# An attention stage in a two-layer encoder: the values matmul with its operands exchanged, two heads on two halves of the array, and the softmax's divisors spread over partitions

## The chip, the cores and the metric

The kernel runs on one core of one Trainium2 chip. A core has a matrix engine (TensorE, PE in the profile, with its weight loads listed apart as PEld), a vector engine (VectorE, DVE), a scalar engine (ScalarE, ACT) and a general engine (GpSimd, POOL); SyncE (SP) issues most of the transfers. Each engine works through its own queue in order, and they wait for each other by semaphores. The metric is the time of one execution on the device in microseconds, lower is better.

## The reference

Two layers; each one takes x of 512 tokens by 1024 features through a half-weighted SwiGLU, a mixer, a second half-weighted SwiGLU and a norm. The mixer has two groups side by side, attention and a causal depthwise convolution of 31 taps, and one output projection over both. What matters here is the end of the attention:

```python
        scores = jnp.where(allowed[None, None], scores, -1e30)
        probs = jax.nn.softmax(scores, axis=-1).astype(vs.dtype)
        outs.append(jnp.einsum('bhqk,bhkd->bqhd', probs, vs))
    ...
    out = jnp.concatenate(outs, axis=1)
    return out.reshape(b, s, h * V_DIM)
    ...
    x = x + jnp.concatenate([attn, conv], axis=-1) @ w_out[l]
```

There are 8 heads with values of 64 columns. Queries come in blocks of 128 tokens; block i sees the keys of blocks 0 to i, with a mask inside the last block. Everything is float32.

## The kernel before

The activations lie transposed, features on partitions and tokens in the free dimension, in tiles of 128x512. Large products keep float32 accuracy by splitting both operands into a high and a low float32r part and adding three matmuls (`mm3`, lines 154 to 156); this fills most of the span. Attention's own small products are single float32 matmuls.

In `mix_body` the attention runs head by head in stages, written down as `ORDER = "t0s1p3v4o5"`: at step n the kernel issues the turning of head n (`turn`, t), the scores of head n-1 (`scores`, s), the turning of the probabilities of head n-3 (`turn_p`, p), the values of head n-4 (`values`, v) and the turning of the output of head n-5 (`turn_out`, o). A scheduler then orders each engine's queue from these and from the convolution, which is issued beside them. So the written order is not the final one.

The stages around the change:

- `scores` makes, for each block of 128 queries, one matmul of up to 512 keys (L834), the mask as a small bf16 matmul (L835), a maximum on DVE (L836) and an exponential on ACT (L840) whose row sums go to `sums`, queries on partitions. The probabilities aren't divided here.
- `turn_p` transposes the probabilities, 10 blocks of 128x128 a head (L855), and copies them out of PSUM on DVE or ACT (L858), so that keys lie on partitions: `pt[j]` holds key block j and the queries of blocks j to 3.
- `values` multiplies them with the values `vs[j]` (L868): for each query block t and key block j up to t, weights are `pt[j]`'s 128 queries, and the moving operand is the head's 64 columns of `vs[j]`. That is 10 matmuls a head. The result has queries on partitions. For an odd head it also makes 1/sum on DVE (`rs`, L873) and multiplies both heads' results by it (`o`, L875).
- `turn_out` transposes the pair's result with four transposes (L886) into a tile with the two heads' features on partitions, and `split` makes its high and low parts (cast on ACT, L161; subtraction on DVE, L162). Four such tiles are the attention's part of the output projection's operand.

The convolution runs over the same stretch. Of four channel blocks two are made on DVE (L922); for the other two ACT makes each tap's product (L926, three buffers) and POOL adds it (L930). When all four are done, POOL adds them up (L944 to L946), PE sums that over the channels (L948), and DVE and ACT normalize. In PE's queue L948 stands before all matmuls of the output projection; the sums of the squares (L198) come two groups of the projection later.

Of the kernel before, what the change touches and what calls it, by code (L numbers as in the profile page):

```python
# [12 lines left out]
ALU = mybir.AluOpType  # L13
AX = mybir.AxisListType

P = 128
# [4 lines left out]
NT = S // P  # L21
# [4 lines left out]
DV = 64  # L26
# [48 lines left out]
def encoder_kernel(ctx: ExitStack, tc: tile.TileContext, xT, consts, vecs, rgain, wgu1, wd1, wdq1,  # L75
# [11 lines left out]
    def nm(s):  # L87
        uid[0] += 1
        return f"{s}{uid[0]}"
# [4 lines left out]
    def tmp(w=S, dt=FP):  # L94
        return tmps.tile([P, w], dt, tag="t", name=nm("t"))

    def bank():
        return psum.tile([P, S], FP, tag="ps", name=nm("ps"))
# [4 lines left out]
    V, A, G, T = nc.vector, nc.scalar, nc.gpsimd, nc.tensor  # L103
# [8 lines left out]
    ident = cst[:, CID:CID + P]  # L112
# [46 lines left out]
    def split(src, made=slot):  # L159
        hi, lo = made(FR), made(FR)  # L160
        order["high"] = A.copy(hi, src).ins  # L161
        order["evicted"] = V.tensor_tensor(lo, src, hi.bitcast(FP), ALU.subtract).ins  # L162
        return hi, lo
# [46 lines left out]
    def spread(r):  # L210

        dg = tmp()
        V.tensor_tensor(dg.rearrange("p (t j) -> p t j", t=NT),
                        ident[:, None, :].to_broadcast([P, NT, P]),
                        r[:, :, None].to_broadcast([P, NT, P]), ALU.mult)
        ps = bank()
        order["spread"] = T.matmul(ps, ones, dg, start=True, stop=True).ins
        return ps
# [398 lines left out]
    def mix_body(kpool, l, gx, norm, done):  # L617
# [28 lines left out]
        cqT, ckT, pq, scqs, vs = [], [], [], [], []  # L646
# [114 lines left out]
        def up_kv(w, t, n=S):  # L761

            ts_ = slice(t * P, (t + 1) * P)
            ps = bank()
            for k in range(2):
                cs = slice(k * n, (k + 1) * n)
                mm3(ps, ckT[k][0][:, ts_], ckT[k][1][:, ts_], w[0][:, cs], w[1][:, cs], k == 0, k == 1)
            return ps
# [33 lines left out]
        at = []  # L802
# [3 lines left out]
        heads = [{} for _ in range(H)]  # L806
# [54 lines left out]
        def values(h):  # L861

            if h % 2 == 0:
                heads[h]["po"] = bank()
            po = heads[h - h % 2]["po"].rearrange("p (t h d) -> p t h d", t=NT, h=2)
            for t in range(NT):
                for j in range(t + 1):
                    T.matmul(po[:, t, h % 2], heads[h]["pt"][j][:, (t - j) * P:(t - j + 1) * P],  # L868
                             vs[j][:, h * DV:(h + 1) * DV], start=j == 0, stop=j == t)
            if h % 2 == 0:  # L870
                return
            rs = small.tile([P, NT, 2], FP, tag="rs", name=nm("rs"))
            V.reciprocal(rs, heads[h - 1]["sums"])  # L873
            o = tmp()
            V.tensor_tensor(o.rearrange("p (t h d) -> p t h d", t=NT, h=2), po,  # L875
                            rs[:, :, :, None].to_broadcast([P, NT, 2, DV]), ALU.mult)
            heads[h]["o"] = o

        def turn_out(h):

            if h % 2 == 0:
                return
            o = heads[h]["o"]
            ps = bank()
            for t in range(NT):
                T.transpose(ps[:, t * P:(t + 1) * P], o[:, t * P:(t + 1) * P], ident)  # L886
            at.append(split(ps, kept if len(at) < 2 else slot))

        STAGES = [({"t": turn, "s": scores, "p": turn_p, "v": values, "o": turn_out}[c], int(d)) for c, d in zip(ORDER[::2], ORDER[1::2])]

        wv = load_w(wkv[l, 1], WC, "uk")
# [4 lines left out]
        with tc.issue_after(order["turned"]):  # L896
            for t in range(NT):
                ps = up_kv(wv, t)
# [5 lines left out]
        for step in range(H + 6):  # L904
            for stage, lag in STAGES:
                h = step - lag
# [7 lines left out]
        for c in range(4):  # L914
# [4 lines left out]
            for k in range(CK - 2, -1, -1):  # L919
# [4 lines left out]
                pr = kpool.tile([P, S], FP, tag="pr", name=nm("pr"), bufs=3)  # L924
# [31 lines left out]
        r = st.token(CW)  # L956
        early_groups(range(E2, E3))
        pr = spread(r)
# [282 lines left out]
```

## Time and profile before

| what | value |
|---|---|
| median of 3 runs | 1804.32 us (1804.24 to 1805.02) |
| profiled execution, its time | 1804.94 us |
| its span | 1803.1 us |
| busy share of the span | PE 99%, DVE 83%, ACT 61%, POOL 23% |

A row of the page's groups or of a timeline reads: line of the kernel, engine, operation, tiles out<-in with their shapes, and how many; then busy time and mean duration, or start and length; then, in brackets or behind a bar, the idle time of the engine just before, and which engine, tile and line ended it. A row of the waits names who waited, for whom, how long in total, how often, and the longest. A row of a stretch gives the engines' busy time with the number of instructions, and then the clock that TensorE was granted, as a share of full speed. The attention stages lie at about 443 to 508 us and 1335 to 1401 us of the span.

### The profile page before, as it was taken

How to read it: one execution, taken by the hardware profiler on the slowest of the kernel's cores; microseconds unless marked ns; L12 is line 12 of the kernel's file. 1: busy time of each engine (PE TensorE's matmuls, PEld its weight loads, DVE VectorE, ACT ScalarE, POOL GpSimd, SP SyncE). 2: the span in 40 equal slices, each digit the busy share in tenths (PEclk: the TensorE clock that was granted, in tenths of full speed). 3: DMA queues.
4: the chain of work that ended last, by engine and by line, in shares of the span. 5: the costliest groups of instructions: out<-in, count | busy, mean ns of one | idle time of the engine just before them, and what ended most of it. 6: DMA issues, size and time to landing. Idle time of an engine off the chain costs nothing. (4 is left out here: it accounts for less than half of the span.)

```text
span 1803.1 us, 29267 instructions
## 1 busy us (share of the span) xinstructions
PE 1781.6 (99%) x11334; PEld 1603.1 (89%) x11334; DVE 1493.0 (83%) x2263; ACT 1091.9 (61%) x1721; POOL 420.2 (23%) x343
## 2 busy tenths in 40 slices
PE   9999999999999999999999999999999999999998
PEld 7899999888788899999888999998978788999997
DVE  7898988689956989898779989876998668989884
ACT  5565656457953575756645656554779435656564
POOL 1000010258943000000310000002689410000102
PEclk9999999999999999999999999999999999999999
DMA  5657574325103466665426575743250125575742
GB/s 167 173 127 182 134 174 125 108 88 136 29 24 100 124 167 160 153 159 129 125 63 169 126 191 122 193 110 111 80 151 3 42 83 161 139 183 134 180 119 74
DMA packets 70412, 226.16 MB, mean 125 GB/s; under 512 B 7936, under 2 KB 8320, under 8 KB 70272
## 3 DMA queue, kind: packets, MB, share of 16 engines
q1 hardware_dynamic: 54000, 169.74, 29.7%
q0 software_dynamic: 16128, 54.53, 17.6%
q8 instruction: 89, 1.46, 0.3%
q14 instruction: 51, 0.42, 0.1%
q10 hardware_dynamic: 144, 0.00, 0.0%
HBM read 222.15 MB, written 2.10 MB: 124 GB/s over the span
## 5 line engine op out<-in xcount | busy, mean ns | idle before, releaser
L155 PE MATMUL ps<-r,wh 128*128 128x256 f32 (+1 forms) x2540 | 805.8, 318 | 0.0
L154 PE MATMUL ps<-r,wh 128*128 128x256 f32 (+1 forms) x2540 | 802.9, 320 | 2.3 <-ACT wh L1060 1.5
L156 PE MATMUL ps<-r,wl 128*128 128x256 f32 (+1 forms) x2348 | 750.0, 321 | 1.7 <-DVE wl L246 1.6
L154 PEld LDWEIGHTS ps<-r,wh 128*128 128x128 f32 x2540 | 480.4, 189 | 44.1 <-ACT wh L138 3.7
L155 PEld LDWEIGHTS ps<-r,wh 128*128 128x128 f32 x2540 | 481.4, 190 | 34.2 <-issue 1.4
L156 PEld LDWEIGHTS ps<-r,wl 128*128 128x128 f32 x2348 | 445.0, 190 | 36.7 <-DVE wl L246 3.2
L373 PE MATMUL ps<-xj,wh 128*128 128x512 f32 x864 | 304.8, 392 | 4.6 <-DVE t L426 4.6
L138 ACT CAST wh<-raw 128x1024 fp32r<-128x1024 f32 (+3 forms) x148 | 132.3, 903 | 203.6 <-PE ps L155 100.3
L390 POOL DMA_DIRECT2D ls<-in_wgu x72 | 62.5, 869 | 734.4 <-ACT ls L389 656.5
L244 ACT CAST wh<-fr 128x1024 fp32r<-128x1024 f32 (+1 forms) x160 | 157.8, 986 | 109.7 <-DVE fr L410 51.3
L144 DVE TENSOR_TENSOR wl<-raw,wh 128x1024 fp32r<-128x1024 f32 (+3 forms) x132 | 145.2, 1108 | 84.7 <-ACT wh L138 84.3
L246 DVE TENSOR_TENSOR wl<-fr,wh 128x1024 fp32r<-128x1024 f32 (+1 forms) x160 | 182.1, 1138 | 20.5 <-ACT wh L244 20.5
L373 PEld LDWEIGHTS ps<-xj,wh 128*128 128x128 f32 x864 | 161.3, 188 | 36.3 <-DVE t L426 6.2
L930 POOL TENSOR_TENSOR y<-y,pr 128x511 f32<-128x511 f32 (+14 forms) x120 | 158.1, 1318 | 54.9 <-ACT pr L926 47.5
L374 PE MATMUL ps<-xj,ls 128*128 128x256 f32 x576 | 161.3, 280 | 0.0
L246 DVE TENSOR_TENSOR wl<-raw,wh 128x1024 fp32r<-128x1024 f32 (+1 forms) x100 | 113.4, 1134 | 14.8 <-ACT wh L244 14.4
L244 ACT CAST wh<-raw 128x1024 fp32r<-128x1024 f32 (+1 forms) x100 | 98.1, 981 | 44.7 <-PE ps L155 27.7
L191 POOL TENSOR_TENSOR r<-r,t 128x512 f32<-128x512 f32 x45 | 75.1, 1678 | 175.7 <-ACT t L187 174.9
L374 PEld LDWEIGHTS ps<-xj,ls 128*128 128x128 f32 x576 | 108.3, 188 | 0.2
L389 ACT ACTIVATE ls<-fr 128x1024 fp32r<-128x1024 f32 (+1 forms) x56 | 56.1, 1001 | 85.3 <-PE ps L374 49.5
L926 ACT ACTIVATE pr<-m,vec 128x511 f32<-128x511 f32 (+14 forms) x120 | 85.8, 737 | 12.4 <-POOL y L930 12.4
L922 DVE SCALAR_TENSOR_TENSOR cv<-m,vec,cv 128x511 f32<-128x511 f32 (+14 forms) x120 | 87.8, 732 | 3.6 <-ACT cv L918 2.2
(242 smaller groups left out, 2926.2 us busy)
## 6 DMA issues: line engine op xcount, KB each, us to landing
fr<-in_wgu SPq DMA_DIRECT2D x112, 512.0 KB, 4.2
ls<-in_wgu POOLq DMA_DIRECT2D x72, 512.0 KB, 6.6
raw<-in_wgu SPq DMA_DIRECT2D x62, 512.0 KB, 4.9
fr<-in_wdq SPq DMA_DIRECT2D x48, 384.0 KB, 5.3
ls<-in_wdq POOLq DMA_DIRECT2D x32, 384.0 KB, 4.7
raw<-in_wd SPq DMA_DIRECT2D x32, 384.0 KB, 3.1
raw<-in_wd SPq DMA_DIRECT2D x32, 256.0 KB, 2.7
raw<-in_wcv SPq DMA_DIRECT2D x16, 512.0 KB, 3.6
```

The lines of the kernel that those rows point to most:

```text
L138: order["cast"] = A.copy(hi[:, :w], raw[:, :w]).ins
L144: (G if kind in POOLW.split() else V).tensor_tensor(lo[:, :w], raw[:, :w], hi[:, :w].bitcast(FP), ALU.subtract)
L154: T.matmul(o, lh, rh, start=first, stop=False, skip_group_check=free)
L155: T.matmul(o, lh, rl, start=False, stop=False, skip_group_check=free)
L156: order["mm"] = T.matmul(o, ll, rh, start=False, stop=last, skip_group_check=free).ins
L244: A.copy(hi[:, :w], src[:, :w])
L246: order["lo"] = V.tensor_tensor(lo[:, :w], src[:, :w], hi[:, :w].bitcast(FP), ALU.subtract).ins
L373: T.matmul(o, w[0][:, c], both, start=start and k == 0, stop=False, skip_group_check=True)
L374: last = T.matmul(o[:, 0:HS], w[1][:, c], both[:, 0:HS], start=False, stop=k == 3, skip_group_check=True).ins
L922: V.scalar_tensor_tensor(acc[:, s:], u[c][:, :S - s], tap(k), acc[:, s:], ALU.mult, ALU.add)
L926: A.activation(pr[:, s:], u[c][:, :S - s], AF.Copy, scale=tap(k))
L930: order["conv"] = G.tensor_tensor(acc[:, s:], acc[:, s:], pr[:, s:], ALU.add).ins
```

## The change

`values` now does nothing for an even head. For an odd one it works on the pair of heads:

- 1/sum (`rs`, queries on partitions) is brought to the result's new layout, features on partitions and queries in the free dimension, by eight float32 matmuls: weights are one column of `rs` repeated 64 times, the moving operand is the identity of 128 columns. Head i of the pair goes to partitions 64i to 64i+63 of a PSUM bank (`pr`). ACT copies the bank to SBUF (`r`).
- The product is made with exchanged operands: weights are the head's 64 columns of `vs[j]`, the moving operand is all of `pt[j]` (512, 384, 256 and 128 queries for j = 0 to 3). The two heads alternate and write the two halves of one bank (`po`).
- DVE multiplies `po` by `r`. The result already has features on partitions, so `turn_out` only splits it, from SBUF; its four transposes and its bank are gone.

```diff
             if h % 2 == 0:
-                heads[h]["po"] = bank()
-            po = heads[h - h % 2]["po"].rearrange("p (t h d) -> p t h d", t=NT, h=2)
-            for t in range(NT):
-                for j in range(t + 1):
-                    T.matmul(po[:, t, h % 2], heads[h]["pt"][j][:, (t - j) * P:(t - j + 1) * P],
-                             vs[j][:, h * DV:(h + 1) * DV], start=j == 0, stop=j == t)
-            if h % 2 == 0:
                 return
             rs = small.tile([P, NT, 2], FP, tag="rs", name=nm("rs"))
             V.reciprocal(rs, heads[h - 1]["sums"])
+            pr = bank()
+            for t in range(NT):
+                for i in range(2):
+                    T.matmul(pr[i * DV:(i + 1) * DV, t * P:(t + 1) * P], rs[:, t, i:i + 1].to_broadcast([P, DV]),
+                             ident, start=True, stop=True)
+            r = tmp()
+            A.copy(r, pr)
+            po = bank()
+            for j in range(NT):
+                for i in range(2):
+                    T.matmul(po[i * DV:(i + 1) * DV, j * P:], vs[j][:, (h - 1 + i) * DV:(h + i) * DV],
+                             heads[h - 1 + i]["pt"][j], start=j == 0, stop=j == NT - 1)
             o = tmp()
-            V.tensor_tensor(o.rearrange("p (t h d) -> p t h d", t=NT, h=2), po,
-                            rs[:, :, :, None].to_broadcast([P, NT, 2, DV]), ALU.mult)
+            V.tensor_tensor(o, po, r, ALU.mult)
             heads[h]["o"] = o
 
         def turn_out(h):
 
             if h % 2 == 0:
                 return
-            o = heads[h]["o"]
-            ps = bank()
-            for t in range(NT):
-                T.transpose(ps[:, t * P:(t + 1) * P], o[:, t * P:(t + 1) * P], ident)
-            at.append(split(ps, kept if len(at) < 2 else slot))
+            at.append(split(heads[h]["o"], kept if len(at) < 2 else slot))
```

## The prediction

> **What bounds the kernel now.** I read the page first, then busy time by stretch, then the timelines of POOL and PE around the end of each attention stage.
>
> ```profile
> span 1803.1 us, 29267 instructions
> PE 1781.6 (99%) x11334; PEld 1603.1 (89%) x11334; DVE 1493.0 (83%) x2263; ACT 1091.9 (61%) x1721; POOL 420.2 (23%) x343
> ```
>
> Over the span TensorE (PE) is the bound. The change, though, lies in two short stages, and there the shares are different (columns: stretch; then PE, PEld, DVE, ACT, POOL busy; granted clock; DMA):
>
> ```profile
> 430.00:520.00 90.00, 87.56 (x553) 71.44 (x552) 74.04 (x134) 68.67 (x147) 72.19 (x57) 1.00 0.24 55
> 1320.00:1420.00 100.00, 97.16 (x585) 78.28 (x584) 82.50 (x148) 74.63 (x156) 74.18 (x58) 0.98 0.22 54
> 460.00:470.00 10.00, 9.24 (x62) 6.61 (x59) 10.00 (x21) 10.00 (x27) 8.34 (x8) 1.00 0.08 16
> 470.00:480.00 10.00, 10.00 (x75) 8.29 (x75) 9.26 (x18) 10.00 (x25) 9.16 (x8) 1.00 0.00 0
> ```
>
> ACT and DVE are full at 460 to 470 and POOL nearly so: POOL adds the taps of the convolution (L930), ACT makes their products (L926) between the softmax's exponentials. POOL's timeline:
>
> ```profile
> 467.90 3.95 POOL L930 TENSOR_TENSOR y<-y,pr 128x508 f32<-128x508 f32 x3 [0.67 <-ACT pr L926]
> 472.23 31.42 POOL L930 TENSOR_TENSOR y<-y,pr 128x505 f32<-128x505 f32 x24 [0.37 <-ACT pr L926]
> 506.29 1.26 POOL L946 TENSOR_TENSOR t<-t,m 128x512 f32<-128x512 f32 x1
> ...
> 1364.24 32.76 POOL L930 TENSOR_TENSOR y<-y,pr 128x506 f32<-128x506 f32 x25 [0.38 <-ACT pr L926]
> 1399.66 1.26 POOL L946 TENSOR_TENSOR t<-t,m 128x512 f32<-128x512 f32 x1
> ```
>
> From 472 and from 1364 POOL runs without a gap to the sum at L946, which ends at 507.55 and at 1400.92. PE's next matmul after attention, L948, reads that sum:
>
> ```profile
> 468.27 2.44 PE L868 MATMUL ps<-m,r 128*128 128x64 f32 x20
> ...
> 507.99 0.66 PE L886 MATMUL ps<-cst,t 128*128 128x128 f32 x4 [0.79 <-DVE t L875]
> 508.48 1.02 PE L948 MATMUL ps<-t,onesm 128*128 128x512 f32 x2
> ...
> 514.92 0.94 PE L198 MATMUL ps<-ones,r 128*128 128x1 f32 x8
> ...
> 1400.97 2.08 PE L948 MATMUL ps<-t,onesm 128*128 128x512 f32 x2 [0.31 <-POOL t L946]
> ...
> 1409.07 0.95 PE L198 MATMUL ps<-ones,r 128*128 128x1 f32 x8
> ```
>
> In layer 1 L948 starts 0.93 us after POOL's end; in layer 2 PE already stands 0.31 us for POOL. All matmuls of the output projection are queued behind L948 on PE, in both programs. So each attention stage has two chains that end together, PE's and POOL's, and PE's can gain at most 0.93 us in layer 1 and nothing in layer 2 unless POOL also ends sooner.
>
> **The change on PE, step by step.** Prices come from back-to-back rows; a plain fp32 matmul stands as two records.
>
> ```profile
> 491.05 0.65 PE L834 MATMUL ps<-r,r 96*128 96x256 f32 x2
> 491.53 0.20 PE L835 MATMUL ps<-mneg,mrow 128*128 128x64 bf16 x1
> 491.57 0.46 PE L834 MATMUL ps<-r,r 96*128 96x128 f32 x2
> 491.87 0.19 PE L835 MATMUL ps<-mneg,mrow 128*128 128x64 bf16 x1
> 491.90 0.89 PE L834 MATMUL ps<-r,r 96*128 96x384 f32 x2
> 492.62 0.19 PE L835 MATMUL ps<-mneg,mrow 128*128 128x64 bf16 x1
> 492.66 1.10 PE L834 MATMUL ps<-r,r 96*128 96x512 f32 x2
> 493.60 0.20 PE L835 MATMUL ps<-mneg,mrow 128*128 128x64 bf16 x1
> ...
> 494.75 2.34 PE L868 MATMUL ps<-m,r 128*128 128x64 f32 x20
> 496.93 0.65 PE L834 MATMUL ps<-r,r 96*128 96x256 f32 x2
> 497.45 0.63 PE L886 MATMUL ps<-cst,t 128*128 128x128 f32 x4
> 497.92 1.04 PE L855 MATMUL ps<-cst,r 128*128 128x128 f32 x8
> ```
>
> *Removed*, for each of the 8 pairs of heads (4 in each layer): 20 values matmuls, 40 records at 2.18/20 = 0.109 us (start at 494.75 to the next start at 496.93), 4.36 us; and four transposes, 0.47 us (497.45 to 497.92). Sum 4.83 us.
>
> *Added*: values with the roles swapped, for both heads matmuls of 512, 384, 256 and 128 columns. The rows give 0.94, 0.72, 0.48 and 0.30 us for these with their first weight load in the open, 4.88 us for two heads; the slope between 512 and 128 columns, (0.94 - 0.30)/384 = 1.67 ns a column, gives 4.27 us for the 2560 columns alone. Then eight spreading matmuls of 128 columns: 8 x 0.30 = 2.40, or 1.71 us by the slope. I take the slope: values of 64 columns, which by it stream for 0.053 us a record, follow each other at 0.109, so it is the load that sets their pace, and streams of 0.107 us and more cover a load of that length. One after another that is 5.98 us, +1.15 us a pair (bounds +1.15 to +2.45). Fully side by side on the two halves it is 2.99 us, -1.84 us a pair. The trace of before has no two matmuls side by side, and every fp32 stream in it takes its full time. What speaks for overlap is the built program: each new matmul carries a tile of 128 by 64 at column 0 or 64, neighbours in the queue alternate, and one head's second record can run beside the other's first. I take side by side, and keep the other end as a rival.
>
> The Trainium skill, "TensorE: Matmul & The Clock Gate" (Part 3: Packing small matmuls), reports 2.38 times for three column tiles of 32, not for fp32. Scaled to two halves, an estimate of about 1.6 times, the pair would take 3.7 us, still 1.1 us less than now, and the sum below stands; no run here shows it yet.
>
> *Where the saving goes.* Four pairs save 7.4 us a layer, of which at most 0.93 can be used; the rest becomes a wait of PE before L948.
>
> **The change on ACT, DVE and POOL.**
>
> ```profile
> L161 ACT CAST m<-ps x4: 574/588/602, 485.4 to 1390.7; 128x512 fp32r<-128x512 f32 x4
> L161 ACT CAST r<-t x96: 602/617/627, 42.2 to 1763.7; 128x512 fp32r<-128x512 f32 x96
> L875 DVE TENSOR_TENSOR t<-ps,rs x8: 680/688/692, 476.4 to 1399.3; 128x512 f32<-128x512 f32 x8
> POOL y L930 <- ACT pr L926: 3.0, 4, 1.4
> ACT pr L926 <- POOL y L930: 2.1, 3, 1.2
> ...
> POOL y L930 <- ACT pr L926: 3.8, 4, 2.1
> ACT pr L926 <- POOL y L930: 1.0, 2, 0.6
> ```
>
> (The wait rows are first of 430 to 520, then of 1330 to 1420.) ACT gets one copy of 128x512 from PSUM per pair, 0.59 us like L161's; the split's cast now reads SBUF, 0.03 us more. DVE's multiply keeps its size and its 0.69 us, so I cost DVE at nothing: PE waited for it only at the stage's last transposes, 0.79 us, and those are gone. The new copy holds what is queued behind it on ACT: exponentials and the taps' products. In the built order three of layer 1's four copies and all four of layer 2's stand ahead of the last tap's product, 1.8 and 2.4 us of ACT's time on the way to POOL. ACT's slack is the time in which it waited for POOL, 2.1 and 1.0 us. If all the slack serves, POOL ends 0 and 1.4 us later; if none, 1.8 and 2.4. I take the middle, 0.9 and 1.9. Then L948 starts at 507.55 + 0.9 = 508.45 in layer 1 (0.0 against before) and 1.9 us later in layer 2.
>
> Values of even heads, which filled PE between scores, move behind the odd head's transposes; PE will stand more often for ACT's exponentials there, but those waits come out of the same saving. The even head's transposed probabilities hold three ring slots a step longer; a late slot would hold up a copy of the next transposes, and I cost that at nothing because PE, which frees the slots, runs early in this case. No DMA changes.
>
> **The clock after the wait.**
>
> ```profile
> 1400.00:1402.00 2.00, 1.68 (x6) 0.93 (x7) 0.68 (x1) 1.28 (x2) 0.92 (x1) 0.72 0.00 0
> 1402.00:1404.00 2.00, 2.00 (x5) 1.30 (x4) 0.92 (x3) 0.98 (x3) 0.00 (x0) 0.50 0.00 0
> 1404.00:1406.00 2.00, 2.00 (x9) 1.61 (x9) 2.00 (x4) 2.00 (x4) 0.00 (x0) 0.93 0.00 0
> ```
>
> In layer 2, after 0.79 and 0.31 us of PE idle, the granted clock fell to 0.50, and L948 to L198 took 8.10 us (1400.97 to 1409.07) where layer 1 took 6.44 (508.48 to 514.92): 1.7 us lost. A wait of some 6 us should bring this to layer 1 too, 1.7 us, and in layer 2 again with up to as much on top; I take half, 0.9.
> The same page of the Trainium skill (Part 1: The HAM clock gate) says that PE falls to half clock after an idle window of some 3.4 us; the 0.50 agrees, though the idle time here was shorter than that window.
>
> **Sum.** 0.0 + 1.9 + 1.7 + 0.9 = +4.5 us on the profiled execution's 1804.94, which is 0.6 above the median of the three runs: 1808.8 us. Its own bounds: -0.9 + 1.4 and the clock's present loss gone, -1.7, gives -1.2, 1803.1; POOL late by 1.8 and 2.4 (0.9 and 2.4 at L948) with twice 1.7 us of clock in layer 1 and 1.7 more in layer 2 gives +8.4, 1812.7.
>
> **Rivals.**
> *The halves run one after another*, so the change doesn't do what it says. PE becomes the later chain: 8 x 1.15 = 9.2 less the 0.31 it now waits, +8.9 us: 1813.2 (1810 to 1816). For it: all of before's fp32 rows. Against: the tiles in the program.
> *The array empties at each change of tile shape.* The row for values
>
> ```profile
> L868 PE MATMUL ps<-m,r x320: 222/275/320, 468.3 to 1398.9; 128*128 128x64 f32 x160
> ```
>
> shows a matmul of 275 ns where starts are 109 ns apart, so about 0.166 us of tail; paid four times a pair (into and out of the halves, twice) it is 0.66 us, 5.3 us in all. Side by side the pair still saves 1.2 us and nothing changes; one after another it makes 1818.5. "TensorEngine Tiling (Array Packing)" of the Trainium skill (Key Properties) states that a change of tiling mode drains TensorE; before has none to show it.
> *Faster.* With fewer values between the scores, ACT gets its scores sooner, POOL's waits on ACT shrink and L946 ends sooner. Most of those waits come before 468.27, the first values matmul, where the order on PE and ACT is the same; only the 0.37 and 0.38 us at 472.23 and 1364.24 are within reach. With them, 0.93, 0.31 and the 1.7 us of clock, all at once: -3.7, 1800.6. It decides only if POOL's end comes earlier by its whole reach, though ACT has more to do.
>
> **How the numbers follow.** POOL-bound with overlap 0.57, serial 0.24, serial with drains 0.12, faster 0.07. A measurement here can tell about 0.2%, 3.6 us. The forecast case reaches from 1803.1 to 1812.7, and I put somewhat under half of it within 0.2%. So faster 0.06, same 0.27, slower 0.67. The range 1802.5 to 1816.5 leaves out most of the drain case and the gain; the forecast's own is 1803.1 to 1812.7.
>
> **What would show it.** Right: rows of the new values lines whose starts lie closer than their streams; a wait of several us before L948 put down to POOL's L946; L946's end near 508.4 and later in layer 2; clock 0.5 after L948 in both layers; the rest of the span unchanged. Wrong: PE without a wait before L948, and values rows of 0.43 us a record end to end (then serial); or POOL's chain ending well before 507.5.

## The result, and the profile after

The changed kernel takes 1812.3 us (median of 5 runs, 1810.24 to 1813.8) where the kernel before takes 1804.32 (1804.02 to 1805.02): a ratio of 1.0042 with a 95% interval of 1.0027 to 1.0057, so it is slower by more than the 0.2% that a measurement here can tell. The prediction said 1808.8, between 1802.5 and 1816.5, so the time lies inside its range. The profiled execution took 1813.8 us, its span 1812.0. From the page:

```profile
span 1812.0 us, 29094 instructions
PE 1777.8 (98%) x11238; PEld 1582.1 (87%) x11238; DVE 1496.1 (83%) x2263; ACT 1095.9 (60%) x1729; POOL 424.4 (23%) x343
```

PE has 3.8 us less to do and POOL 4.2 us more, although not one of POOL's instructions was changed. PE's timeline in both attention stages:

```profile
443.50 0.60 PE L811 MATMUL ps<-cst,q 128*96 128x128 f32 x4
...
497.25 1.09 PE L870 MATMUL ps<-cst,rs 128*64 128x128 f32 x16
498.18 2.32 PE L877 MATMUL ps<-r,m 128*64 128x512 f32 x16
500.43 1.31 PE L855 MATMUL ps<-cst,r 128*128 128x128 f32 x10
...
509.76 2.08 PE L948 MATMUL ps<-t,onesm 128*128 128x512 f32 x2 [4.84 <-POOL t L946]
519.03 0.95 PE L198 MATMUL ps<-ones,r 128*128 128x1 f32 x8
...
1341.22 0.60 PE L811 MATMUL ps<-cst,q 128*96 128x128 f32 x4
...
1408.59 2.08 PE L948 MATMUL ps<-t,onesm 128*128 128x512 f32 x2 [6.14 <-POOL t L946]
1417.34 0.95 PE L198 MATMUL ps<-ones,r 128*128 128x1 f32 x8
```

A pair's spreading and values matmuls (L870, L877) take 3.18 us from their first start to the start of what follows (497.25 to 500.43), where values and transposes took 4.83 by the same measure. PE is done early, and then stands for 4.84 and 6.14 us in front of L948, each time for POOL's L946. The stage's own clock starts at its first L811. In the kernel before those are:

```profile
443.79 0.60 PE L811 MATMUL ps<-cst,q 128*96 128x128 f32 x4
1335.81 0.60 PE L811 MATMUL ps<-cst,q 128*96 128x128 f32 x4
```

So L948 stood 64.69 and 65.16 us into the stage (508.48 - 443.79, 1400.97 - 1335.81), and stands now at 66.26 and 67.37: 1.57 and 2.2 us later. From L948 to L198 it took 6.44 and 8.10 us and takes 9.27 and 8.75: 2.83 and 0.65 us more. That is +7.3 us of the span's +8.9. The rest lies outside the attention stages, in front of the first (-0.3), between the two (+1.3) and behind the second (+0.6). Those stretches vary by as much among other kernels that contain the change: from L198 of layer 1 to the first L811 of layer 2 one of the variants below took 819.5 us and another 822.3, so I don't put that to the change.

POOL's timeline shows why L948 is late:

```profile
472.73 3.92 POOL L930 TENSOR_TENSOR y<-y,pr 128x505 f32<-128x505 f32 x3 [0.96 <-ACT pr L926]
477.05 28.42 POOL L930 TENSOR_TENSOR y<-y,pr 128x502 f32<-128x502 f32 x21 [0.40 <-ACT pr L926]
505.44 1.26 POOL L944 TENSOR_TENSOR t<-m,y 128x512 f32<-128x512 f32 x1
506.77 1.59 POOL L945 TENSOR_TENSOR t<-t,y 128x512 f32<-128x512 f32 x1
508.44 1.26 POOL L946 TENSOR_TENSOR t<-t,m 128x512 f32<-128x512 f32 x1
```

Two things are new. Where POOL waited once for 0.37 us it waits twice, 0.96 and 0.40 (in layer 2 once for 0.38, and now 0.94 and 0.39). And four single additions a layer take 1.54 to 1.64 us where all the others from 477 on take 1.20 to 1.27: L945 here, three more inside the long row, and four in layer 2. The groups of L162, DVE's subtraction in the split, in before (the first two) and in after (columns: count, shortest, median and longest in ns, first and last start):

```profile
L162 DVE TENSOR_TENSOR m<-ps,m x2: 680/680/681, 486.9 to 500.0; 128x512 fp32r<-128x512 f32 x2
L162 DVE TENSOR_TENSOR r<-ps,r x2: 692/692/692, 505.7 to 509.3; 128x512 fp32r<-128x512 f32 x2
```

```profile
L162 DVE TENSOR_TENSOR m<-t,m x2: 1164/1182/1201, 481.7 to 493.8; 128x512 fp32r<-128x512 f32 x2
L162 DVE TENSOR_TENSOR r<-t,r x2: 837/1106/1376, 503.0 to 506.4; 128x512 fp32r<-128x512 f32 x2
```

L162 read the turned output in PSUM (`ps`) and the high part in SBUF. Since there is nothing left to turn, it reads the product `t` in SBUF and the high part in SBUF. It takes 0.84 to 1.38 us instead of 0.68. Each of the eight stretched additions of POOL starts while an L162 runs, 0.3 to 0.9 us behind its start (L945 at 506.77 behind 506.41); in the kernel before additions run beside L162 as well, and none is stretched. Whether the one is the cause of the other the two traces can't tell; an experiment below does.

The granted clock behind L948 in layer 1 (stretch; PE, PEld, DVE, ACT, POOL busy; clock; DMA):

```profile
508.00:510.00 2.00, 0.24 (x1) 0.24 (x2) 0.00 (x0) 0.20 (x1) 1.63 (x2) 0.70 0.00 0
510.00:512.00 2.00, 2.00 (x3) 0.94 (x4) 0.13 (x1) 0.00 (x0) 0.00 (x0) 0.50 0.03 8
512.00:514.00 2.00, 2.00 (x6) 1.55 (x5) 2.00 (x4) 1.38 (x3) 0.00 (x0) 0.50 0.00 0
```

It is 0.50 from 510 to 514 and still 0.59 up to 516; the kernel before had no drop here.

### The profile page after: what moved, and what is told of

It is laid out like the page before. It is cut to its first block, busy times and chain, and to the rows that moved or that the text cites. A ratio compares the mean times of both kernels' runs of the same rounds, so it can differ in the third digit from the quotient of the medians.

```text
span 1812.0 us, 29094 instructions
## 1 busy us (share of the span) xinstructions
PE 1777.8 (98%) x11238; PEld 1582.1 (87%) x11238; DVE 1496.1 (83%) x2263; ACT 1095.9 (60%) x1729; POOL 424.4 (23%) x343
## 5 line engine op out<-in xcount | busy, mean ns | idle before, releaser
L926 ACT ACTIVATE pr<-m,vec 128x511 f32<-128x511 f32 (+14 forms) x120 | 87.1, 752 | 11.3 <-POOL y L930 11.3
L390 POOL DMA_DIRECT2D ls<-in_wdq x32 | 27.6, 862 | 269.7 <-ACT ls L389 269.7
```

Source lines behind the costliest of these rows:

```text
L390: G.dma_start(out=lo[:, :n], in_=w, accum_op=ALU.add)
L926: A.activation(pr[:, s:], u[c][:, :S - s], AF.Copy, scale=tap(k))
```

## The experiments

The theory after the two traces: the halves do run side by side; POOL's chain sets the end; POOL is later because of L162's two SBUF operands and of a product that ACT hands over later; and the wait that PE's own saving makes costs again through the clock. Rivals: the halves run one after another after all; ACT's new copies of r delay POOL (the prediction's own reason); POOL's end doesn't matter. In this table "mean" is the start of the last mean matmul (L948) after the stage's first L811, "to L198" the time from there, both for layers 1 and 2 and taken before rounding, so up to 0.01 off the rows. Kernels in one block shared the runs of the kernel before on one chip, whose median stands in its row.

| kernel | median us | ratio to before, 95% interval | mean | to L198 |
|---|---|---|---|---|
| before (with the first result) | 1804.32 | | 64.69, 65.16 | 6.43, 8.09 |
| changed | 1812.3 | 1.0042 [1.0027, 1.0057] | 66.26, 67.36 | 9.26, 8.76 |
| before (first block) | 1803.7 | | | |
| serial | 1815.31 | 1.0062 [1.0047, 1.0077] | 69.52, 70.69 | 6.53, 6.53 |
| rdve | 1811.62 | 1.0043 [1.0027, 1.0060] | 66.18, 67.75 | 6.53, 8.73 |
| warm2 | 1806.49 | 1.0017 [1.0007, 1.0026] | 66.07, 67.33 | 6.53, 6.53 |
| poolcut | 1803.7 | 1.0004 [0.9995, 1.0014] | 63.36, 64.77 | 6.53, 9.17 |
| before (second block) | 1804.09 | | | |
| opsum | 1809.54 | 1.0027 [1.0018, 1.0037] | 64.91, 66.00 | 8.08, 8.99 |
| e1_1 | 1810.45 | 1.0032 [1.0021, 1.0044] | 66.90, 67.47 | 5.88, 5.98 |
| opsum_e1 | 1808.49 | 1.0020 [1.0011, 1.0030] | 66.52, 66.01 | 5.78, 5.89 |
| b_e1 | 1812.11 | 1.0037 [1.0024, 1.0049] | 67.50, 67.50 | 5.88, 5.88 |
| before (third block) | 1803.31 | | | |
| ow | 1805.06 | 1.0009 [1.0001, 1.0018] | 64.88, 65.98 | 6.53, 8.09 |
| best | 1805.15 | 1.0012 [1.0003, 1.0021] | 65.19, 64.59 | 7.02, 8.03 |
| b_best | 1813.42 | 1.0060 [1.0047, 1.0074] | 68.76, 68.78 | 7.45, 8.39 |
| before (fourth block) | 1803.48 | | | |
| best2 | 1800.54 | 0.9981 [0.9972, 0.9989] | 62.51, 63.59 | 6.52, 6.53 |

Between blocks I compare ratios; 0.001 is 1.8 us. By the intervals, a difference of two kernels' ratios is clear of noise from about 0.002 on; smaller ones rest on the traces, and each trace is one execution.

### serial: the two heads one after the other

```diff
-            for t in range(NT):
-                for i in range(2):
+            for i in range(2):
+                for t in range(NT):
                     T.matmul(pr[i * DV:(i + 1) * DV, t * P:(t + 1) * P], ...
...
-            for j in range(NT):
-                for i in range(2):
+            for i in range(2):
+                for j in range(NT):
                     T.matmul(po[i * DV:(i + 1) * DV, j * P:], ...
```

> The changed kernel, with the loop over the two heads outside the loop over the blocks in both new groups of matmuls, so that neighbours in PE's queue use the same half. Theory (the halves do run side by side, and PE has 4.84 and 6.14 us to spare before L948): a pair costs PE about 6.0 us where it now takes 3.3, 2.7 us more, 10.7 us a layer; that is more than the wait, so PE becomes the later chain, L948 comes 5.9 and 4.5 us later, the wait before it and the half clock behind it go (about 5 us back): 1812.3 + 10.4 - 5 = about 1818. Rival (which half is written does not matter, PE's time per pair is set elsewhere): 1812, wait and pair as they are.

PE's timeline at a pair in layer 1:

```profile
488.70 1.58 PE L870 MATMUL ps<-cst,rs 128*64 128x128 f32 x16
490.87 3.93 PE L877 MATMUL ps<-r,m 128*64 128x512 f32 x16
...
512.69 1.13 PE L948 MATMUL ps<-t,onesm 128*128 128x512 f32 x2 [0.68 <-POOL t L946]
```

The same 16 records of L877 take 3.93 us in this order and 2.32 in the changed kernel's, and the spreading 1.58 against 1.09. So the changed kernel's halves overlap, and the order of issue decides it: here neighbours in the queue have to belong to different halves. The time rises by 3.6 us by the ratios (barely clear of noise), where some 6 were forecast, and L948 comes 3.3 us later than in the changed kernel in both layers, where 5.9 and 4.5 were. Against before it comes 4.8 and 5.5 us later, though a pair's two rows are at most 0.7 us longer than the 4.83 us removed (1.58 + 3.93; the rival's forecast was +1.15). POOL is late with it, by its waits from 443 to 512 (who, for whom, total, times, longest):

```profile
POOL y L930 <- ACT pr L926: 8.3, 10, 1.6
```

In the changed kernel that row reads 3.6 us in 5 waits. In that stretch ACT stands for PE's L855, L811 and L870, 3.5 us in three waits that the changed kernel's list doesn't have, and so its products come late. This coupling the prediction's rival (1813.2) had left out; how much of it belongs to which wait I haven't taken apart. The clock did not drop here, where PE waits 0.68 us in layer 1 and 1.85 in layer 2.

### rdve: the copy of r on VectorE

```diff
-            A.copy(r, pr)
+            V.tensor_copy(r, pr)
```

> The changed kernel, with the copy r made by DVE in place of ACT. Theory (ACT's four copies and their places hold up the taps' products): POOL's last add comes 0.5 to 2 us sooner in each layer, L948 with it: 1809 to 1811. Rival (the taps are late through the order of the exponentials on ACT, not through the copies): 1812. Rival (DVE is as full as ACT between 460 and 490, and the maxima wait instead): 1813 or more.

POOL's chain ends as late as before the edit: the mean is at 66.18 and 67.75 (66.26 and 67.36 with the copies on ACT), and POOL's two waits are still there (0.95 and 0.40). So the copies of r are not what delays POOL, and the prediction's reason for its late end falls.

### warm2: filler matmuls into the wait

```diff
-        T.matmul(pm, onesm, ysum, start=True, stop=True)
+        with tc.issue_after(heads[H - 1]["v"]):
+            for _ in range(5):
+                T.matmul(pm, ones, x[:, 0, :], start=True, stop=True)
+        order["mean"] = T.matmul(pm, onesm, ysum, start=True, stop=True).ins
...
-        early_groups(range(E1, E2))
+        with tc.issue_after(order["mean"]):
+            early_groups(range(E1, E2))
```

(`"v"` is the last values matmul; the lines behind the cut keep the projection's first groups behind the mean.)

> The changed kernel, with five fp32 matmuls of 512 columns, whose result is written over and not used, put between the last values matmul and L948, so that PE is busy for 4.3 us of its wait. Theory (the wait costs only by the half clock behind it): L948 starts when it did, the granted clock behind it stays at 1.00, L948 to L198 takes 6.4 us in both layers (9.27 and 8.76 now): 1812.3 - 2.8 - 2.3 = about 1807. Rival (the slow matmuls behind L948 have another cause): 1812 and the same distances.

PE's timeline, and then one of the stretches:

```profile
504.30 4.56 PE L950 MATMUL ps<-x,ones 128*128 128x512 f32 x10
509.24 1.13 PE L951 MATMUL ps<-t,onesm 128*128 128x512 f32 x2 [0.38 <-POOL t L946]
```

```profile
510.00:512.00 2.00, 2.00 (x9) 1.49 (x8) 1.60 (x3) 0.85 (x2) 0.00 (x0) 1.00 0.00 0
```

Nothing useful was added, the mean starts where it did, and the ratio falls by 0.0025, 4.5 us: the clock stays at 1.00 and the way to L198 shrinks by 2.73 and 2.23 us. The half clock behind the wait is shown, at about 5 us for the two layers; 1.6 us of it (8.09 against 6.53) layer 2 had before the change too.

### poolcut: two of POOL's three additions left out

```diff
-        G.tensor_tensor(ysum, ys[0], ys[1], ALU.add)
-        G.tensor_tensor(ysum, ysum, ys[2], ALU.add)
-        (G if YP else V).tensor_tensor(ysum, ysum, ys[3], ALU.add)
+        G.tensor_tensor(ysum, ys[2], ys[3], ALU.add)
```

> The changed kernel, with two of POOL's three adds before L948 left out (the mean over channels takes two of the four blocks). Theory (L948 is set by POOL's chain): its end and L948 come 2.5 us sooner in each layer, 1812.3 - 5 = 1807, and less if the shorter wait (2.3 and 3.6 us) spares the clock, down to 1803. Rival (PE or ACT sets the end of the stage): 1812.

The mean over the channels now lacks two of the four blocks. L948's counterpart comes 2.9 and 2.6 us earlier, about the 2.5 to 2.7 us that two additions last, and the ratio falls by 0.0038, 6.9 us, to that of the kernel before: POOL's chain sets the end. Layer 1's clock is spared besides, layer 2's is not.

### opsum: the product kept in PSUM

```diff
-            o = tmp()
-            V.tensor_tensor(o, po, r, ALU.mult)
-            heads[h]["o"] = o
+            V.tensor_tensor(po, po, r, ALU.mult)
+            heads[h]["o"] = po
```

> Edit: the changed kernel, but VectorE's product of the values with 1/sum is written back into the PSUM bank of the values, so that the split's subtraction (L162) again reads one operand from PSUM and one from SBUF, as it did in the kernel before; the computation is the same. Theory A (a VectorE subtraction with both operands in SBUF stretches the POOL addition that it overlaps, four times a layer): the four POOL additions of 1.5 to 1.7 us go back to 1.22 us, L162 goes from 1.16-1.38 back to about 0.7 us, POOL ends and the mean matmul L948 starts 1.3 us earlier in each layer (about 65.0 and 66.1 us after the stage's first L811 instead of 66.3 and 67.4), and the time is about 1812.3 - 2.6 = 1809.7. Theory B (POOL is late for another reason: what ACT hands it, or the copies of r): additions as long as before, L948 where it was, 1812 within 1. Theory C: the longer hold of the PSUM bank delays TensorE, and the time rises to some 1814.

L162 again, by its two groups, and POOL's row that answers to the 28.42 us above:

```profile
L162 DVE TENSOR_TENSOR m<-ps,m x2: 677/678/679, 481.5 to 494.0; 128x512 fp32r<-128x512 f32 x2
L162 DVE TENSOR_TENSOR r<-ps,r x2: 691/691/691, 502.2 to 505.4; 128x512 fp32r<-128x512 f32 x2
```

```profile
476.87 26.16 POOL L929 TENSOR_TENSOR y<-y,pr 128x502 f32<-128x502 f32 x20 [0.39 <-ACT pr L925]
```

The same mathematics and the same engines; only the first operand of L162 lies in PSUM. L162 is back at 0.68 us, 20 additions take 26.16 us (1.31 us apiece with what lies between them, against 28.42/21 = 1.35 without the edit), none of them over 1.3 us, the mean starts 1.35 and 1.36 us earlier, and the ratio falls by 0.0015, 2.7 us (not clear of noise by itself). Theory A held on every number it gave.

The rows also show who waits for whom. VectorE's L162 beside POOL's L944 and L945 in the changed kernel, and then one from rdve with the addition beside it:

```profile
506.41 0.84 DVE L162 TENSOR_TENSOR r<-t,r 128x512 fp32r<-128x512 f32 x1 [0.68 <-ACT r L161]
```

```profile
480.98 0.68 DVE L162 TENSOR_TENSOR m<-t,m 128x512 fp32r<-128x512 f32 x1
481.02 1.75 POOL L930 TENSOR_TENSOR y<-y,pr 128x499 f32<-128x499 f32 x1
```

The first L162 starts while L944 runs (505.44 to 506.70) and ends 0.55 us behind it; L945, which starts while L162 runs, ends 1.12 us behind L162. All eight L162 of the changed kernel start while an addition runs and end 0.55 us behind that addition, and the next addition ends 1.06 to 1.12 us behind L162. In rdve's rows the subtraction starts between two additions: it takes its 0.68 us, and the addition that starts 0.03 us later takes 1.75 instead of 1.25. So whoever starts first pays nothing, and the other waits for it; in the changed kernel both pay, because POOL's additions follow each other within 0.1 us and each subtraction starts into one. Two SBUF operands alone cost nothing: the kernel before has 120 such L162, none of them beside an addition, and each takes 0.68 or 0.69 us.

In the Trainium skill, "SBUF — State Buffer" (section "Who interferes with whom") says that a VectorE instruction with two SBUF inputs contends with a GpSimd instruction that reads SBUF, because its second input comes through the read interface the two share, that this contention is an exclusive lock, and that issue order decides who blocks. The traces agree; the size here is +0.3 to +0.4 us for an addition of some 1.22 us and +0.2 to +0.7 us for the subtraction of 0.68.

What is left of POOL's lateness, 1.1 and 0.8 us (64.86 - 63.76 and 65.95 - 65.11 at the end of the last addition), goes with the 0.96 and 0.40 us of waits, which serial, rdve, warm2, poolcut and opsum show too. ACT's timeline at that place, before and after:

```profile
471.31 1.38 ACT L926 ACTIVATE pr<-m,vec 128x505 f32<-128x505 f32 x2
472.54 0.73 ACT L813 ACTIVATE r<-ps,gqs 96x512 f32<-96x512 f32 x1
```

```profile
471.24 0.75 ACT L813 ACTIVATE r<-ps,gqs 96x512 f32<-96x512 f32 x1
471.82 1.38 ACT L926 ACTIVATE pr<-m,vec 128x505 f32<-128x505 f32 x2
```

The eviction of the next turned queries (L813) now stands ahead of two products for POOL instead of behind them: the even head's values no longer hold PE, so the turn (L811) starts at 468.19 instead of 471.07, and the scheduler puts its eviction first. That is read off the order of the rows (layer 2 has the same swap at 1368.73 and 1369.31); no kernel tried it alone, so this part of the cause is argued and not shown.

### e1_1, opsum_e1 and b_e1: a projection group ahead of the mean

```diff
-E1 = 0
+E1 = 1
```

The same edit of the changed kernel, of opsum and of the kernel before.

> Edit: the changed kernel with one of the output projection's early groups (12 matmuls of 0.23 us, 2.8 us) issued ahead of the mean matmul L948, into the 4.84 and 6.14 us that TensorE waits there; nothing is computed otherwise. Theory (TensorE's saving is real, and is lost in front of L948, whose wait for POOL all projection matmuls queue behind): the wait in front of L948 falls by about 2.8 us in each layer, L948 itself stays where it is, the half clock after it (about 5 us for both layers) goes for the most part, and the time is between 1812.3 - 5.6 - 5 = 1802 and 1807. Rival (the chain behind L948, mean, squares, token sum, is what counts, and TensorE only lacks work afterwards): L948 to L198 does not get shorter by more than the clock's part, and the time stays at 1808 to 1812.

> Edit: both: the product kept in PSUM, and one projection group ahead of L948. If the two add up: 1.3 us a layer below the kernel with the early group alone, some 1799 to 1804, so at or below the kernel before (1804.3). If TensorE is the later of the two once POOL ends sooner, the product in PSUM is worth under 1 us here.

> Edit: the kernel before with the same early group ahead of L948, as the control. There TensorE waits only 0.79 and about 1 us ahead of L948, so a group of 2.8 us put there delays L948 by about 2 us a layer and takes as much from the work that covers the chain behind it: 1804.3 to 1808. If it is faster than 1802, the early group is worth something of its own, and what it brings the changed kernel is not the saving of this change.

All three missed. PE in the first:

```profile
503.21 1.02 PE L877 MATMUL ps<-r,m 128*64 128x512 f32 x2
504.17 0.50 PE L154 MATMUL ps<-m,wh 128*128 128x512 f32 x1
...
505.76 2.37 PE L877 MATMUL ps<-r,m 128*64 128x512 f32 x14
...
511.22 1.02 PE L948 MATMUL ps<-t,onesm 128*128 128x512 f32 x2
517.10 1.02 PE L198 MATMUL ps<-ones,r 128*128 128x1 f32 x8 [2.08 <-DVE r L191]
```

The scheduler put half of the group ahead of the last pair's values, so the last split came later, the group waited for it, and L948 behind it came 0.64 us later although POOL was done. And the group is missing behind L948: PE now waits 2.08 us at L198. By the ratios it brings 1.8 us of the changed kernel's 7.6, which is not clear of noise, and opsum_e1 4.0. Their traces are the quickest execution of e1_1 (1807.28 us) and the slowest of opsum_e1 (1813.32), so the two can't be set beside each other. The control is slower than the kernel before by 6.7: there the group stands whole where it was written, ahead of L948, which comes 2.8 and 2.3 us later, and the clock drops behind the 2.07 us in front of L198.

### ow: product in PSUM and fillers together

opsum with four of warm2's fillers.

> Edit: both causes at once: the changed kernel with the product kept in PSUM (as in opsum) and four filler matmuls of 0.91 us between the last values and the mean matmul (their results are not used). If the change's loss is made of these two things, POOL's stretched additions and the half clock after TensorE's wait, nothing but the one late tap is left: the mean matmul at some 64.9 and 66.0 us of the stage, 6.00 us from it to L198 in both layers, and 1809.5 - 5.3 = 1804.2 (1803 to 1806), the time of the kernel before. Above 1807, a third cause is open.

1805.06 us, 1.0009 [1.0001, 1.0018] of before: 1.6 us, from 0.2 to 3.2 by the interval. The time came as forecast, the 6.00 us to L198 did not (6.53 and 8.09). The mean is 0.2 and 0.8 us later than in before, as in opsum. The fillers end too early in layer 2, PE still waits 1.92 us there, and that layer keeps its clock drop (8.09, as in before). So L162's operand and the clock make up all but 1.6 us of the change's loss of 7.6, and the late products on ACT, 1.1 and 0.8 us at POOL's end, can account for that.

### best, b_best and best2: a shorter POOL chain

```diff
-        G.tensor_tensor(ysum, ys[0], ys[1], ALU.add)
-        G.tensor_tensor(ysum, ysum, ys[2], ALU.add)
-        (G if YP else V).tensor_tensor(ysum, ysum, ys[3], ALU.add)
+        G.tensor_tensor(ysum, ys[1], ys[2], ALU.add)
         pm = bank()
-        T.matmul(pm, onesm, ysum, start=True, stop=True)
+        with tc.issue_after(heads[H - 1]["v"]):
+            T.matmul(pm, onesm, ys[0], start=True, stop=False)
+            T.matmul(pm, onesm, ys[3], start=False, stop=False)
+            order["mean"] = T.matmul(pm, onesm, ysum, start=False, stop=True).ins
...
-        early_groups(range(E1, E2))
+        with tc.issue_after(order["mean"]):
+            early_groups(range(E1, E2))
```

This is best2, on top of opsum. best, and b_best on top of the kernel before, have a VectorE addition of the channels 0 and 3 (L933; L934 in b_best) and one matmul in place of the first two.

> Edit: the product kept in PSUM, and POOL's chain shortened: one of the three additions (channels 0 and 3) goes to VectorE, reading its PSUM accumulator, one is replaced by a second accumulating mean matmul on TensorE, and one stays on POOL; same computation. Theory (the saving of the change on TensorE is real and was hidden by POOL): POOL ends 2.5 us earlier in each layer, at about 62.3 and 63.4 us, the second mean matmul starts there, TensorE waits for it only some 0.7 and 1.9 us, the clock drop goes in layer 1 and halves in layer 2: about 1800.5 (1798 to 1804), faster than the kernel before. Rival (the chain behind the mean, or DVE's extra addition, takes the gain): 1804 to 1808.

> Edit: the kernel before with the same shorter POOL chain, as the control. There TensorE's values and turns end at 63.4 us, and the first of the two mean matmuls adds 1.0, so the second starts at 64.4 us in both layers, bound by TensorE, where L948 stood at 64.69 and 65.16: 1.1 us gained, and about 1.0 us of the clock in layer 2: 1802.3 (1801 to 1804). The difference to the kernel above, about 2 us, is what the change is worth once POOL no longer sets the end; if this control is as fast or faster, the change is worth nothing here.

> Edit: as best, but the channels 0 and 3 go into the mean by two accumulating matmuls of their own on TensorE, behind the last values, in place of VectorE's late addition (L933, which TensorE waited 2.90 us for); POOL keeps one addition; same computation. Theory (POOL's chain, the stretched additions and the wait it makes on TensorE are the whole loss, and the saving on TensorE is real): POOL ends at about 62.2 and 63.7 us of the stage as in best, TensorE's values at 60.5, its two filler means at 62.4, the last mean starts at 62.4 and 63.8, 2.3 us ahead of the kernel before in layer 1 and 1.4 in layer 2; the waits ahead of the first mean and the last are 0 and at most 1.3 us, so 6.00 us follow to L198 in layer 1 and 6 to 7 in layer 2. Time about 1801 (1799 to 1803.5), below the kernel before on the same chip by some 2 us. Rival: what follows the mean waits for the split of the last pair instead, and the time stays at 1804 to 1806.

best and b_best were spoiled by a piece of their own, PE's row in best:

```profile
507.24 2.04 PE L949 MATMUL ps<-r,onesm 128*128 128x512 f32 x2 [2.90 <-DVE r L933]
```

The scheduler put VectorE's addition behind the last split, and the clock was down by then. So b_best says nothing on what the shorter chain is worth to the kernel before. best2 does without that addition; PE's timeline in layer 1 and layer 2:

```profile
502.51 2.32 PE L877 MATMUL ps<-r,m 128*64 128x512 f32 x16
504.77 1.12 PE L946 MATMUL ps<-m,onesm 128*128 128x512 f32 x2
505.73 1.02 PE L947 MATMUL ps<-m,onesm 128*128 128x512 f32 x2
506.61 1.13 PE L948 MATMUL ps<-t,onesm 128*128 128x512 f32 x2
...
1399.07 1.12 PE L948 MATMUL ps<-t,onesm 128*128 128x512 f32 x2 [1.17 <-POOL t L943]
...
1405.60 0.95 PE L198 MATMUL ps<-ones,r 128*128 128x1 f32 x8
```

The mean is 2.2 and 1.6 us ahead of the kernel before, and layer 2's way to L198 is 6.53 us instead of 8.10. The time is 1800.54 us, 0.9981 [0.9972, 0.9989] of the kernel before, as forecast (1801). It beats the changed kernel clearly; against the kernel before the interval lies below 1, but the 0.19% is just under the 0.2% named above. With PE's values still ending at 63.4 us of the stage, as in before, the two extra means (0.96 and 0.88 us) would have carried the last one to 65.2; by that sum PE's saving is used here. A control with exactly this edit on the kernel before was not run, and how much of the 2.9 us it would get is open.

## Why the prediction was right in sign and short in size

- *PE, side by side or not*: right. Taken at 2.99 us a pair, measured 3.18 (497.25 to 500.43), against 4.83 removed; the estimate from "TensorE: Matmul & The Clock Gate" (Part 3) of the Trainium skill, 3.7 us, was 0.5 too long. The rival of serial halves is excluded by the 2.32 against 3.93 us of the serial kernel, although its 1813.2 us lay nearer to the measured time than the forecast: the time alone could not have told them apart. The rival of drains: the whole pair takes 0.19 us more than its streams side by side, so no tail of 0.66 us shows.
- *The saving isn't usable because L948 waits for POOL*: right; it became 4.84 and 6.14 us of wait, and poolcut shows that POOL's chain sets the end.
- *POOL's end*: forecast +0.9 and +1.9 us, measured +2.45 and +2.2 against the stage's start. The size in layer 2 is near by luck, the reason wrong in both. The copies of r on ACT cost POOL nothing that can be seen (rdve). Two other things did: L162's two SBUF operands, 1.35 us a layer (opsum), and, by the order of the rows alone, the place of L813 ahead of L926, about 1 us.
- *The step that failed*: "DVE's multiply keeps its size and its 0.69 us, so I cost DVE at nothing". The multiply did; the split behind it changed the place of one operand, was priced for ACT's cast (0.03 us) and never for DVE's subtraction and what runs beside it. That L162's operand moves from PSUM to SBUF stood in the change.
- *L948*: 0.0 and +1.9 forecast, +1.57 and +2.2 measured: 1.9 us of the miss, from that step and ACT's order, less the cost of the copies that didn't come.
- *The clock*: forecast 1.7 and 0.9 us, measured 2.83 and 0.65, in sum 2.6 against 3.5: right in kind (warm2), 0.9 us short.
- *Sum*: +4.5 forecast, +7.3 in the two stages of the traces, +7.6 by the ratio. The 0.3 us between these two is within what a measurement can't tell.
- *Faster*, the rival, needed POOL's 0.37 and 0.38 us of waiting to shrink; they grew to two waits, 0.96 and 0.40 in layer 1 and 0.94 and 0.39 in layer 2. A kernel ahead of the one before came only when POOL's chain itself was cut (best2).

## What to carry to other kernels

When a stage has two chains that end together, shortening one turns into a wait, and here the wait cost again through the clock; cut the other chain too, or put work of the other chain into the wait, as best2 does. When a step that moved data between PSUM and SBUF goes away, look at every later instruction that read its result: an operand that moves to SBUF can slow an engine that isn't part of the change at all. Before an experiment's edit is blamed, read where the scheduler put it: four of these twelve kernels (e1_1, opsum_e1, best and b_best) missed for an order that nobody wrote.

## What the runs showed that was not expected

- Whether two float32 matmuls with 64 columns of weights run side by side hangs on the issue order: 2.32 us when the halves alternate, 3.93 when one head follows the other, for the same 16 records.
- VectorE's subtraction and POOL's addition take turns when both of the subtraction's operands lie in SBUF: the later one ends 0.55 us (subtraction) or 1.06 to 1.12 us (addition) behind the earlier one.
- The clock falls after waits of very different length. It stayed at 1.00 behind waits of 1.17 us (best2, layer 2), 1.96 (poolcut, layer 1), 2.08 (e1_1, at L198) and 2.34 (rdve, layer 1), and fell to 0.50 behind 0.79 and 0.31 us (before, layer 2), 1.92 (ow, layer 2), 1.97 (opsum_e1, at L198), 2.07 (b_e1, at L198), 2.09 (b_best) and every wait of 2.9 us or more. In this range the length of the last wait alone doesn't decide; what does, no run here tells. Executions of one kernel differ too: e1_1's mean granted clock goes from 0.997 to 0.999 over its six, and the traced one, without a drop, is at 0.999.
